# A hybrid decoder on one core: the operands of RWKV's key projection formed in another order, and another order in its recurrence's step

## The chip, the cores and the metric

The kernel runs on one core of a Trainium2 chip. The metric is device time in microseconds (us) of the whole program, median of three runs. The engines are PE (TensorE, matmuls; PEld loads their weights), DVE (VectorE), ACT (ScalarE), POOL (GpSimd) and SP (SyncE, which here only issues DMAs). Each engine takes its instructions in the order of its own queue; a DMA is issued from the queue of SP or ACT and can only be issued when what it waits for has come.

## What is computed

Two decoder layers over x of 1024 tokens by 1024 channels, in float32. The even layer (gMLP and dilated attention) isn't touched. The odd layer is RWKV-7 time mixing:

```python
xx = concat([zeros, h[:, :-1]]) - h
xr, xw, xk, xv, xa, xg = [h + xx * mu[i] for i in range(6)]
r, k, v, g = xr @ w_r, xk @ w_k, xv @ w_v, xg @ w_g
logw = -softplus(-(w0 + tanh(xw @ w1) @ w2)) - 0.5
decay = exp(-exp(logw))
a = sigmoid(a0 + (xa @ a1) @ a2)
kk = hs(k * k_k);  kk = kk * rsqrt(max(sum(kk * kk), 1e-24))     # per head of 64
k = k * (1.0 + (a - 1.0) * k_a)
# per head, over the tokens t:
sa = state @ -kk_t
state = state * w_t + sa (x) (kk_t * a_t) + v_t (x) k_t
y_t = state @ r_t
# then a norm over each head, a bonus sum(r * k * r_k) * v, times silu(g), @ w_o, residual, final norm
```

## The kernel before

Matrices are multiplied in float32 precision by splitting both operands in a high part and a rest (`xh`, `xl`; `wh`, `wl`; the weights' rest is formed by L106, the activations' by L740 on POOL or DVE) and adding three products (`mm3`, L153). The odd layer runs as a plan of twelve chunks `j`: r (j 0 to 3), k (4 to 7), v (8 to 11), each of 256 output columns. r and k are channel-major: a **unit** is one block of 128 channels `p` and one half `f` of 512 tokens, 24 matmuls of 512 columns. v is token-major, 768 matmuls of 256 columns. Before a projection its input is mixed (`mixed`: a scale on ACT L736, one operation on DVE L737, the high part on ACT, the rest L740). `mixed_out` does the same for the second half of the gate's input and stores it in DRAM; it stands at j = 6 (`XD`), in k's projection.

For every unit of k, `Prep` takes the matmuls' result and forms the operands of the recurrence. Matmuls with the small weights `w2`, `a2` (L795, L796) give the decay and a, tanh is on ACT (L797), a running sum over each chunk of 64 tokens is a scan on DVE (L802), its exponentials `E`, `En` are on ACT. From these and k come `AR` (L809, L811, L812) and `BK` (L813, L814, L817), from k and a the product L816 on POOL and the bonus L820. Two matmuls with a selection matrix `sel` sum over the channels of a head (L822, L823); their result is copied to `so` (L825) and stored in two pieces. AR and BK go to DRAM. In this part of the program a scheduler sets the order within each engine.

The recurrence works in chunks of 64 tokens (`c`), two per step (block `b`): 8 blocks, of which a start, six steps and an end are written out by hand as lists of names (`SCAN_START`, `SCAN_STEP`, `SCAN_END`); for all engines and SP the order is then that of the lists. What the names issue: `U` solves for a chunk (PE, copied by ACT to UV, L1250); `st` multiplies into the state (PE L1271) and adds it to S (DVE L1273); `keep` decays S (POOL L1262); `W`, `Y` are the products with the state. Ahead of the step, for later chunks: `ld` loads A and BK; `sc`, `al` form the chunk's score matrices MY, M and AK; `msk` masks MY (L1078) and AK (L1080) on POOL; `dec` decays BK (POOL L1062); `T` transposes it. The triangular inverse of a block is found partly by rows on DVE: `sM` stores M (L1055, issued by ACT), `lM` loads it as Nt in another layout, `ip`, `ia`, `ie` form its diagonal blocks, each count of `ib` issues one piece of its rows (L1153 to L1160), `ic` stores the rows as XT (L1167, SP), `lX` loads them as X (L1175, SP), and `mx`, `ma`, `mb` merge them on PE (L1193, L1206). `uv` loads v into UV, `Yd` stores Y (L1298, issued by ACT). `g` issues a piece of the gate projection (PE L943), stored to `sg_d` (L950).

Of the kernel before, what the change touches and what calls it, by code (L numbers as in the profile page):

```python
# [42 lines left out]
XD = 6  # L43
# [712 lines left out]


class Prep:


    def __init__(self, g, a, pool):
# [3 lines left out]
        self.w2 = {}  # L765

    def second(self, p):

        if p not in self.w2:
            g, nc = self.g, self.g.nc  # L770
            self.w2 = {p: []}
            for n in ("rw_w2", "rw_a2"):
# [8 lines left out]
        return self.w2[p]

    def __call__(self, p, f, pk):
        g, nc, pool = self.g, self.g.nc, self.pool
        sl = slice(f * 512, (f + 1) * 512)
        kk, rk = g.pr[:, 8, p:p + 1], g.pr[:, 10, p:p + 1]
        c3 = lambda t: t.rearrange("p (c t) -> p c t", t=CH)
        ks = pool.tile([P, 512], F32, name="ks", bufs=2)
        nc.scalar.activation(ks, pk, AF.Copy)  # L789
# [4 lines left out]
        for i, ((wh, wl), src, b) in enumerate(zip(self.second(p), (self.TH, self.UA), (g.w0h, g.a0h))):  # L794
            nc.tensor.matmul(pz[:, i], wh, src[:, sl], start=True, stop=False)  # L795
            nc.tensor.matmul(pz[:, i], wl, src[:, sl], start=False, stop=True)  # L796
# [3 lines left out]
        L = pool.tile([P, 512], F32, name="L", bufs=2)  # L800
        E = tw
        nc.vector.tensor_tensor_scan(L, g.smask.rearrange("p c t -> p (c t)"), tw, 0.0, op0=OP.mult, op1=OP.add)  # L802
# [6 lines left out]
        nc.vector.scalar_tensor_tensor(AR[:, :, 0, 1:CH], c3(ks)[:, :, 1:CH], kk, E3[:, :, 0:CH - 1],  # L809
                                       op0=OP.mult, op1=OP.mult)  # L810
        nc.vector.tensor_scalar(AR[:, :, 0, 0:1], c3(ks)[:, :, 0:1], kk, None, op0=OP.mult)  # L811
        (nc.vector if p % 2 else nc.gpsimd).tensor_tensor(AR[:, :, 1, :], c3(rt), E3, OP.mult)  # L812
        nc.vector.scalar_tensor_tensor(BK[:, :, 0, :], c3(ta), 1.0, c3(ks), op0=OP.add, op1=OP.mult)  # L813
        nc.vector.scalar_tensor_tensor(BK[:, :, 0, :], BK[:, :, 0, :], g.kkn[:, p:p + 1], En, op0=OP.mult, op1=OP.mult)  # L814
        nc.vector.tensor_scalar(ta, ta, g.kah[:, p:p + 1], g.kam[:, p:p + 1], op0=OP.mult, op1=OP.add)
        nc.gpsimd.tensor_tensor(ta, ta, ks, OP.mult)  # L816
# [3 lines left out]
        nc.vector.scalar_tensor_tensor(ta, rt, rk, ta, op0=OP.mult, op1=OP.mult)  # L820
        pss = g.bC([64, 512], "pt")
        nc.tensor.matmul(pss[0:32], g.sel, sq, start=True, stop=True)  # L822
        nc.tensor.matmul(pss[32:64], g.sel, ta, start=True, stop=True)  # L823
        so = pool.tile([64, 512], F32, name="so", bufs=1)
        nc.vector.tensor_copy(so, pss)  # L825
        nc.sync.dma_start(g.ss_d[:, p, sl], so[0:2])
        nc.sync.dma_start(g.bo_d[:, p, sl], so[32:34])
# [4 lines left out]


def odd_layer(g, a, hT, wt, out):
# [34 lines left out]
    mixed(g, hT, 0, (1,), xn)  # L869
    for j, (i, W, fn, ld, ev, c) in enumerate(plan):  # L870
        if c == 0:
# [11 lines left out]
        if j == XD:  # L883
            mixed_out(g, hT, 5, 1, g.xg_d)
# [676 lines left out]
```

## Time and profile before

| | us |
|---|---|
| median of three runs | 1486.93 (1485.79 to 1487.78) |
| the profiled execution | 1486.46 |
| its span, from the first to the last recorded instruction | 1484.4 |
| PE busy in the span | 1305.9 |
| DVE, ACT, POOL busy | 913.4, 628.8, 544.7 |

Busy time says how much of the span an engine worked, not what it was waiting for. The odd layer lies after about 640 us: r to 728, k with its operands to about 938, v to 997, the start of the recurrence to 1082, six steps with U at 1082.7, 1121.6, 1158.3, 1192.0, 1228.0 and 1263.9, and the end.

### The profile page before, as it was taken

How to read it: one execution, taken by the hardware profiler on the slowest of the kernel's cores; microseconds unless marked ns; L12 is line 12 of the kernel's file. 1: busy time of each engine (PE TensorE's matmuls, PEld its weight loads, DVE VectorE, ACT ScalarE, POOL GpSimd, SP SyncE). 2: the span in 40 equal slices, each digit the busy share in tenths (PEclk: the TensorE clock that was granted, in tenths of full speed). 3: DMA queues.
4: the chain of work that ended last, by engine and by line, in shares of the span. 5: the costliest groups of instructions: out<-in, count | busy, mean ns of one | idle time of the engine just before them, and what ended most of it. 6: DMA issues, size and time to landing. Idle time of an engine off the chain costs nothing.

```text
span 1484.4 us, 30909 instructions
## 1 busy us (share of the span) xinstructions
PE 1305.9 (88%) x12773; PEld 1110.6 (75%) x12773; DVE 913.4 (62%) x1489; ACT 628.8 (42%) x1188; POOL 544.7 (37%) x353
## 2 busy tenths in 40 slices
PE   5899999799998999999998869998977878687877
PEld 5887788788896799978854537896766667567877
DVE  8741536663556436760698997332676776668884
ACT  4421535543554324652555554232434444354322
POOL 8750102030213512221343353023744444367751
PEclk9999999899999999999999989998988998889999
DMA  6277446240543435133187547427675565675412
GB/s 220 86 265 188 114 128 171 72 128 15 148 108 115 141 106 152 47 110 108 50 243 196 132 118 196 105 74 218 167 234 157 154 156 145 160 220 212 145 34 95
DMA packets 253276, 209.16 MB, mean 141 GB/s; under 512 B 79648, under 2 KB 215424, under 8 KB 253136
## 3 DMA queue, kind: packets, MB, share of 16 engines
q1 hardware_dynamic: 230336, 191.98, 44.4%
q10 hardware_dynamic: 22800, 15.21, 3.7%
q8 instruction: 100, 1.64, 0.5%
q14 instruction: 40, 0.33, 0.1%
HBM read 135.71 MB, written 71.43 MB: 140 GB/s over the span
## 4 chain that ended last, share of the span: by engine, by line
PE 51%; DVE 17%; DMA 12%; ACT 7%; issue 6%; POOL 4%; SPq 2%; ACTq 1%; DVEq 0%; POOLq 0%
PE pj L153 33%; PE pj L943 3%; PE pt L572 2%; PE pj L1473 2%; PE pj L711 2%; DMA X<-XT 1%; DMA XT<-xm 1%; DMA w<-in_rw_a_dram 1%; DMA BK<-BK_d 1%; PE ch L1271 1%; PE op L580 1%; ACT wh L105 1%; PE sp L559 1%; PE sp L562 1%; ACT UV L1250 1%
## 5 line engine op out<-in xcount | busy, mean ns | idle before, releaser
L106 POOL TENSOR_TENSOR wl<-wraw,wh 128x1024 fp32r<-128x1024 f32 x38 | 95.6, 2518 | 174.2 <-ACT wh L105 161.5
L153 PE MATMUL pj<-hh,wh 128*128 128x512 f32 x320 | 127.3, 398 | 0.0
L153 PE MATMUL pj<-hh,wl 128*128 128x512 f32 x320 | 126.7, 396 | 0.0
L153 PE MATMUL pj<-hl,wh 128*128 128x512 f32 x320 | 126.6, 396 | 0.0
L106 DVE TENSOR_TENSOR wl<-wraw,wh 128x1024 fp32r<-128x1024 f32 x46 | 71.7, 1564 | 84.7 <-ACT wh L105 44.0
L105 ACT ACTIVATE wh<-wraw 128x1024 fp32r<-128x1024 f32 x84 | 88.2, 1057 | 66.0 <-DMA wraw<-in_w_in_even_dram 23.3
L153 PE MATMUL pj<-xl,wh 128*128 128x512 f32 x256 | 104.2, 408 | 2.5 <-DVE xl L740 2.5
L153 PE MATMUL pj<-xh,wh 128*128 128x512 f32 x256 | 103.8, 408 | 2.5 <-ACT ks L789 2.5
L153 PE MATMUL pj<-xh,wl 128*128 128x512 f32 x256 | 103.6, 405 | 0.2 <-POOL wl L106 0.2
L566 DVE CUSTOM_DVE_ANT_0 sc<-sp,tb 128x128 f32<-128x128 f32 (+3 forms) x64 | 48.2, 754 | 58.0 <-PE sp L562 49.6
L1473 PE MATMUL pj<-wh,yl 128*128 128x256 f32 x256 | 74.1, 289 | 6.4 <-POOL yl L106 6.4
L1473 PE MATMUL pj<-wh,yh 128*128 128x256 f32 x256 | 74.8, 292 | 5.2 <-DVE x L1477 5.2
L153 PE MATMUL pj<-wh,hh 128*128 128x256 f32 x256 | 74.7, 295 | 2.9 <-ACT hh L265 2.6
L737 DVE SCALAR_TENSOR_TENSOR xm<-hT,pr,xm 128x512 f32<-128x512 f32 x56 | 49.0, 917 | 44.1 <-ACT xm L736 43.7
L153 PE MATMUL pj<-wh,hl 128*128 128x256 f32 x256 | 74.8, 293 | 1.2 <-DVE hl L266 1.2
L153 PE MATMUL pj<-wh,yl 128*128 128x256 f32 x256 | 73.8, 288 | 1.9 <-POOL yl L624 1.9
L153 PE MATMUL pj<-wl,hh 128*128 128x256 f32 x256 | 74.3, 291 | 0.0
L1473 PE MATMUL pj<-wl,yh 128*128 128x256 f32 x256 | 73.8, 288 | 0.0
L153 PE MATMUL pj<-wh,yh 128*128 128x256 f32 x256 | 73.3, 286 | 0.5 <-ACT yh L623 0.5
L153 PE MATMUL pj<-wl,yh 128*128 128x256 f32 x256 | 72.9, 285 | 0.0
L153 PE MATMUL pj<-wh,xh 128*128 128x256 f32 x256 | 72.2, 282 | 0.1
L153 PE MATMUL pj<-wl,xh 128*128 128x256 f32 x256 | 72.2, 282 | 0.0
(320 smaller groups left out, 4063.2 us busy)
## 6 DMA issues: line engine op xcount, KB each, us to landing
wraw<-in_w_in_even_dram SPq DMA_DIRECT2D x28, 512.0 KB
tb<-tb SPq DMA_DIRECT2D x16, 512.0 KB
A_d<-AR SPq DMA_DIRECT2D x16, 512.0 KB
wraw<-in_rw_wg_dram SPq DMA_DIRECT2D x16, 512.0 KB
A<-A_d SPq DMA_DIRECT2D x16, 512.0 KB
BK<-BK_d SPq DMA_DIRECT2D x16, 512.0 KB
xt<-in_x_dram SPq DMA_DIRECT2D x8, 512.0 KB
dv<-vt SPq DMA_DIRECT2D x16, 256.0 KB
```

The source lines that it names most:

```text
L105: nc.scalar.activation(hi, raw, AF.Copy)
L106: sub.tensor_tensor(lo, raw, hi.bitcast(F32), OP.subtract)
L153: nc.tensor.matmul(ps, a(k), b(k), start=(n == 0), stop=(n == 3 * KT - 1))
L559: nc.tensor.matmul(sp[:, c0:c1], qs[:, b * P:(b + 1) * P], kh[:, c0:c1], start=True, stop=False)
L562: nc.tensor.matmul(sp[:, c0:c1], qs[:, b * P:(b + 1) * P], kl[:, c0:c1], start=False, stop=True)
L566: nc.vector.tensor_tensor_reduce(sc[:, :n], sp[:, :n], tb[:, off:off + n], 1.0, BIG, OP.add, OP.min, mn)
L572: nc.tensor.transpose(pt[:, j - j0, :], sc[:, j * P:(j + 1) * P], g.ident)
L580: nc.tensor.matmul(op[:, s0:QW], vt[:, j, :], pth[j // 4][:, j % 4, s0:QW], start=(j == 0), stop=False)
L711: nc.tensor.matmul(ps, x[:, 2 * kk + i, :], y[:, i, o:o + 512], start=(n == 0), stop=(n == 47))
L737: nc.vector.scalar_tensor_tensor(t, hT[kk, f][:, j, 0:512], g.pr[:, i, k:k + 1], t, op0=OP.mult, op1=OP.add)
L943: nc.tensor.matmul(ps, u[:, k], v[:, k % 2], start=(k == 0 and i == 0), stop=(k == KT - 1 and i == 2))
L1473: nc.tensor.matmul(ps[:, i, :], u[:, k], v[:, k % 4], start=(k == 0 and j == 0), stop=(k == KT - 1 and j == 2))
```

## The change

*In k's projection.* The small weights are loaded and split once for a chunk of 256 columns, and each unit's call is divided: `gates` (matmuls, tanh, scan, exponentials, the parts of BK that need no k) is issued ahead of the unit's own matmuls, `operands` after them, and `sum`, the two matmuls with `sel`, after the matmuls of the next unit. `sel` is wider and is shifted by p, so that the sums of all eight p add up in one bank per half and are copied and stored once. E has a leading column of ones, so that AR's first column needs no operation of its own; two operations move to ACT (bias and scale); the product of k with En becomes POOL's. For j = 4 to 7 the order on PE is that of the code. `mixed_out` moves to v's chunks, two of eight parts after each.

*In the recurrence.* `msk` is divided: `mA` (AK, this block's chunks) and `mY` (MY, two chunks later in the program than before). The rows of the inverse stand ahead of the second state update. M's and Y's stores are issued by SP. v is loaded a chunk earlier. The gate's pieces stand at other places.

```diff
-    "U0 al0 ib2 st0 al1 sM0 uv0 Y0 keep1 ib1 W1 sc0 ib1 U1 uv1 ld6 st1 sc1 ib1 ic0 dec0 Y1 lM0 W2 keep2 ip0 lX0 "
-    "gx1 sc2 Yd0 T0 msk0 g2 ia0 sc3 g2 mx0 ma0 ie0 g2 dec1 T1 mb0 msk1 g3 ib3 ld7 gl2")
+    "U0 al0 ib2 st0 al1 Y0 uv1 keep1 mA0 mA1 W1 sM0 sc0 ib3 ld6 U1 sc1 g1 mY0 mY1 ic0 st1 dec0 lM0 Y1 g1 W2 keep2 "
+    "ip0 lX0 gx1 uv2 sc2 Yd0 T0 g1 sc3 ia0 ld7 mx0 ma0 dec1 ie0 g2 mb0 g2 T1 g2 ib3 gl2")
...
+    def project(self, x, w, c, fs=(0, 1)):
...
+                t = self.gates(2 * c + m, f)
+                ps = g.bA([P, 512], "pj")
+                mm3(g.nc, ps, lambda k: wh(k, m), lambda k: wl(k, m),
+                    lambda k: x[0][k // 2, f][:, k % 2, 0:512], lambda k: x[1][k // 2, f][:, k % 2, 0:512])
+                self.sum()
+                self.operands(2 * c + m, f, ps, *t)
...
-        nc.vector.scalar_tensor_tensor(AR[:, :, 0, 1:CH], c3(ks)[:, :, 1:CH], kk, E3[:, :, 0:CH - 1],
-                                       op0=OP.mult, op1=OP.mult)
-        nc.vector.tensor_scalar(AR[:, :, 0, 0:1], c3(ks)[:, :, 0:1], kk, None, op0=OP.mult)
-        (nc.vector if p % 2 else nc.gpsimd).tensor_tensor(AR[:, :, 1, :], c3(rt), E3, OP.mult)
-        nc.vector.scalar_tensor_tensor(BK[:, :, 0, :], c3(ta), 1.0, c3(ks), op0=OP.add, op1=OP.mult)
-        nc.vector.scalar_tensor_tensor(BK[:, :, 0, :], BK[:, :, 0, :], g.kkn[:, p:p + 1], En, op0=OP.mult, op1=OP.mult)
-        nc.vector.tensor_scalar(ta, ta, g.kah[:, p:p + 1], g.kam[:, p:p + 1], op0=OP.mult, op1=OP.add)
-        nc.gpsimd.tensor_tensor(ta, ta, ks, OP.mult)
-        nc.vector.tensor_tensor(BK[:, :, 1, :], c3(ta), En, OP.mult)
...
+        nc.scalar.activation(BK[:, :, 0, :], ta.rearrange("p (c t) -> p c t", t=CH), AF.Identity,
+                             bias=g.kkn[:, p:p + 1], scale=g.kkn[:, p:p + 1])
+        nc.scalar.activation(ta, ta, AF.Identity, bias=g.kam[:, p:p + 1], scale=g.kah[:, p:p + 1])
...
+        kt = pool.tile([P, 512], F32, name="kt", bufs=1)
...
+        nc.gpsimd.tensor_tensor(BK[:, :, 1, :], c3(ks), c3(En), OP.mult)
+        nc.gpsimd.tensor_tensor(kt, ta, ks, OP.mult)
+        nc.vector.scalar_tensor_tensor(AR[:, :, 0, :], c3(ks), kk, E[:, :, 0:CH], op0=OP.mult, op1=OP.mult)
+        nc.vector.scalar_tensor_tensor(kt, rt, rk, kt, op0=OP.mult, op1=OP.mult)
+        (nc.vector if p % 2 else nc.gpsimd).tensor_tensor(AR[:, :, 1, :], c3(rt), E[:, :, 1:CH + 1], OP.mult)
+        nc.vector.tensor_tensor(BK[:, :, 0, :], BK[:, :, 0, :], BK[:, :, 1, :], OP.mult)
+        nc.vector.tensor_tensor(BK[:, :, 1, :], c3(ta), BK[:, :, 1, :], OP.mult)
...
+        nc.tensor.matmul(ps[0:32], g.sel[:, 7 - p:39 - p], sq, start=p == 0, stop=p == KT - 1)
+        nc.tensor.matmul(ps[32:64], g.sel[:, 7 - p:39 - p], ta, start=p == 0, stop=p == KT - 1)
...
+            order.enter_context(tc.manual_schedule(engines={mybir.EngineType.PE}))
...
-        if j == XD:
-            mixed_out(g, hT, 5, 1, g.xg_d)
...
+        if j >= 8:
+            mixed_out(g, hT, 5, 1, g.xg_d, (2 * j - 16, 2 * j - 15))
...
-            self.g.nc.scalar.dma_start(self.g.MA_d[b2][k].rearrange("c q t s -> t (c q) s"),
+            self.g.nc.sync.dma_start(self.g.MA_d[b2][k].rearrange("c q t s -> t (c q) s"),
...
-            self.g.nc.scalar.dma_start(self.g.Y_d[b].rearrange("(c t) h d -> t c h d", c=2)[:, :, 8 * e:8 * e + 8],
+            self.g.nc.sync.dma_start(self.g.Y_d[b].rearrange("(c t) h d -> t c h d", c=2)[:, :, 8 * e:8 * e + 8],
```

DVE's queue in the middle of k's projection, before: the operations of one unit, whose factors are in `tz_7465` and `L_7487`, from the first scaling to the bonus (numbers behind names are buffers).

```order
L799 TENSOR_SCALAR tz_7465<-tz_7465 128x512
L825 COPY so_7427<-pt_7424 64x512
L802 SCALAR_TENSOR_TENSOR L_7487<-smask_4820,tz_7465 128x512
L813 SCALAR_TENSOR_TENSOR BK_7493<-tz_7465,ks_7460 128x8x64
L815 TENSOR_SCALAR tz_7465<-tz_7465,kah_4810,kam_4812 128x512
L809 SCALAR_TENSOR_TENSOR AR_7492<-ks_7460,pr_4802,tz_7465 128x8x63
L812 TENSOR_TENSOR AR_7492<-rl_7462,tz_7465 128x8x64
L811 TENSOR_SCALAR AR_7656<-ks_7624,pr_4802 128x8
L779 TENSOR_TENSOR rw_w2l_7714<-w2_7710,rw_w2h_7713 128x128
L814 SCALAR_TENSOR_TENSOR BK_7493<-BK_7493,kkn_4808,L_7487 128x8x64
L817 TENSOR_TENSOR BK_7493<-tz_7465,L_7487 128x8x64
L820 SCALAR_TENSOR_TENSOR tz_7465<-rl_7462,pr_4802,tz_7465 128x512
```

The same engine and stretch, after: the unit whose factors are in `tz_7212`, with its AR in `AR_7259`, its BK in `BK_7224` and its bonus in `kt_7258`.

```order
L814 TENSOR_SCALAR tz_7212<-tz_7212 128x512
L842 TENSOR_TENSOR BK_7162<-tz_7150,BK_7162 128x8x64
L815 SCALAR_TENSOR_TENSOR tz_7212<-smask_4820,tz_7212 128x512
L839 SCALAR_TENSOR_TENSOR kt_7196<-rl_7147,pr_4802,kt_7196 128x512
L840 TENSOR_TENSOR AR_7259<-rl_7209,E1_6010 128x8x64
L838 SCALAR_TENSOR_TENSOR AR_7259<-ks_7254,pr_4802,E1_6010 128x8x64
L841 TENSOR_TENSOR BK_7224<-BK_7224 128x8x64
L814 TENSOR_SCALAR tz_7283<-tz_7283 128x512
L842 TENSOR_TENSOR BK_7224<-tz_7212,BK_7224 128x8x64
L815 SCALAR_TENSOR_TENSOR tz_7283<-smask_4820,tz_7283 128x512
L839 SCALAR_TENSOR_TENSOR kt_7258<-rl_7209,pr_4802,kt_7258 128x512
```

The unit's bonus product now stands behind the scaling and the scan of the next unit (`tz_7283`), and its AR and BK take four operations where they took seven.

DVE's queue in the recurrence's step, before, from the step's first row pieces (products of Nt and the rows found so far, and their sums) to the last, around the two state updates S:

```order
L1153 TENSOR_TENSOR tm<-Nt,xm 128x864
L1155 TENSOR_REDUCE R<-tm 128x3x12
L1273 TENSOR_TENSOR S<-ch,S 128x512
L1153 TENSOR_TENSOR tm<-Nt,xm 128x864
L1155 TENSOR_REDUCE R<-tm 128x3x12
L1153 TENSOR_TENSOR tm<-Nt,xm 128x576
L1155 TENSOR_REDUCE R<-tm 128x2x12
L1273 TENSOR_TENSOR S<-ch,S 128x512
L1158 TENSOR_TENSOR tm<-DN,R 128x768
L1160 TENSOR_REDUCE xm<-tm 128x12x8
```

And after:

```order
L1199 TENSOR_TENSOR tm<-Nt,xm 128x864
L1201 TENSOR_REDUCE R<-tm 128x3x12
L1319 TENSOR_TENSOR S<-ch,S 128x512
L1199 TENSOR_TENSOR tm<-Nt,xm 128x864
L1201 TENSOR_REDUCE R<-tm 128x3x12
L1199 TENSOR_TENSOR tm<-Nt,xm 128x576
L1201 TENSOR_REDUCE R<-tm 128x2x12
L1204 TENSOR_TENSOR tm<-DN,R 128x768
L1206 TENSOR_REDUCE xm<-tm 128x12x8
L1319 TENSOR_TENSOR S<-ch,S 128x512
```

The second update of S has moved from ahead of the last row piece to behind it.

SP's queue in one step, before: the loads of v, then A and BK, the rows' store and the loads of the inverse.

```order
L1013 DMA UV<-v_d 64x512 x4
L1001 DMA A<-A_d 128x1024
L1003 DMA BK<-BK_d 128x1024
L1167 DMA XT_139<-xm 1024x1x32 x2
L1095 DMA Nt<-MA_132 64x1024 x2
L1175 DMA X<-XT_139 32x16x32 x4
L1001 DMA A<-A_d 128x1024
L1003 DMA BK<-BK_d 128x1024
```

And after:

```order
L1055 DMA UV<-v_d 64x512 x2
L1097 DMA MA_132<-M 32x16x32 x4
L1043 DMA A<-A_d 128x1024
L1045 DMA BK<-BK_d 128x1024
L1213 DMA XT_139<-xm 1024x1x32 x2
L1141 DMA Nt<-MA_132 64x1024 x2
L1221 DMA X<-XT_139 32x16x32 x4
L1055 DMA UV<-v_d 64x512 x2
L1344 DMA Y_146<-Y 64x2x512 x2
L1043 DMA A<-A_d 128x1024
L1045 DMA BK<-BK_d 128x1024
```

M's and Y's stores now stand in this queue; v's loads are parted, and the second of them and Y's store stand behind X.

More of the change, by code (lines that the diff above doesn't have):

```diff
@@ L41 @@
 NT = 4
-XD = 6
 GR = 9
@@ L741, in mixed, with mixed_out @@
             xh[kk, f], xl[kk, f] = h, l
-def mixed_out(g, hT, i, f, dst):
+def mixed_out(g, hT, i, f, dst, ks):
     nc = g.nc
-    for k in range(KT):
+    for k in ks:
         src = hT[k // 2, f][:, k % 2]
@@ L783, in __call__ @@
-    def __call__(self, p, f, pk):
-        g, nc, pool = self.g, self.g.nc, self.pool
[L785 to L789, printed above, removed]
+        self.E = [pool.tile([P, 8, CH + 1], F32, name=f"E{i}") for i in range(2)]
+        for E in self.E:
+            g.nc.vector.memset(E[:, :, 0:1], 1.0)
@@ new lines, in __init__, with second @@
+        self.w2, self.sums, self.n = {}, {}, 0
+        self.due = None
+    def second(self, c):
+        if c not in self.w2 and c < D // CB:
+            g, nc = self.g, self.g.nc
+            raw = g.s2([P, 2, CB], F32, "w2")
+            for i in range(2):
+                for j, n in enumerate(("rw_w2", "rw_a2")):
+                    nc.sync.dma_start(raw[64 * i:64 * i + 64, j], self.a[n][0][:, c * CB:(c + 1) * CB])
+            hi = self.pool.tile([P, 2, CB], F32R, name="w2h", bufs=2)
+            lo = self.pool.tile([P, 2, CB], F32R, name="w2l", bufs=2)
+            nc.scalar.activation(hi, raw, AF.Copy)
+            nc.vector.tensor_tensor(lo, raw, hi.bitcast(F32), OP.subtract)
+            self.w2[c] = hi, lo
@@ new lines, in project @@
+    def project(self, x, w, c, fs=(0, 1)):
+        g = self.g
+        wh, wl = w
+        self.second(c)
+        for f in fs:
+            for m in range(2):
+                t = self.gates(2 * c + m, f)
[4 more added lines that the diff above has]
+                self.operands(2 * c + m, f, ps, *t)
+            if f == 0:
+                self.second(c + 1)
@@ L790, in __call__, with gates @@
+    def gates(self, p, f):
+        g, nc, pool = self.g, self.g.nc, self.pool
+        sl, o = slice(f * 512, (f + 1) * 512), slice((p % 2) * P, (p % 2 + 1) * P)
+        wh, wl = self.w2[p // 2]
         rt = pool.tile([P, 512], F32, name="rl", bufs=2)
@@ L793, in __call__ @@
         tz = pool.tile([P, 2, 512], F32, name="tz", bufs=2)
[L794 to L796 removed]
+        for i, (src, b) in enumerate(((self.TH, g.w0h), (self.UA, g.a0h))):
+            nc.tensor.matmul(pz[:, i], wh[:, i, o], src[:, sl], start=True, stop=False)
+            nc.tensor.matmul(pz[:, i], wl[:, i, o], src[:, sl], start=False, stop=True)
             nc.scalar.activation(tz[:, i], pz[:, i], AF.Tanh, bias=b[:, p:p + 1], scale=0.5)
@@ L821, in __call__ @@
[L821 to L827, printed above, removed]
+        nc.vector.tensor_tensor_scan(tw, g.smask.rearrange("p c t -> p (c t)"), tw, 0.0, op0=OP.mult, op1=OP.add)
@@ L831, in __call__, with sum @@
             nc.sync.dma_start(g.BK_d[64:128, f * 8:(f + 1) * 8, p, 1 - j], BK[64:128, :, j])
+    def sum(self):
+        if self.due is None:
+            return
+        g, nc = self.g, self.g.nc
+        (p, f, sq, ta), self.due = self.due, None
+        if p == 0:
+            self.sums[f] = g.bC([64, 512], "pt")
+        ps = self.sums[f]
+        nc.tensor.matmul(ps[0:32], g.sel[:, 7 - p:39 - p], sq, start=p == 0, stop=p == KT - 1)
+        nc.tensor.matmul(ps[32:64], g.sel[:, 7 - p:39 - p], ta, start=p == 0, stop=p == KT - 1)
+        if p == KT - 1:
+            sl = slice(f * 512, (f + 1) * 512)
+            so = g.s2([64, 512], F32, "xm")
+            nc.vector.tensor_copy(so, ps)
+            nc.sync.dma_start(g.ss_d.rearrange("e q s -> (e q) s")[:, sl], so[0:16])
+            nc.sync.dma_start(g.bo_d.rearrange("e q s -> (e q) s")[:, sl], so[32:48])
 def odd_layer(g, a, hT, wt, out):
@@ L869, in odd_layer @@
     mixed(g, hT, 0, (1,), xn)
+    order = ExitStack()
     for j, (i, W, fn, ld, ev, c) in enumerate(plan):
+        if j == 3:
+            prep.second(0)
+        if j == 4:
+            order.enter_context(tc.manual_schedule(engines={mybir.EngineType.PE}))
+        if j == 8:
+            prep.sum()
+            order.close()
         if c == 0:
@@ L1073, in transposed, with mask_AK, mask_MY @@
                 nc.scalar.activation(BKT[:, 4 * q:4 * q + 4], pt, AF.Copy)
-    def masks(self, c):
+    def mask_AK(self, c):
+        nc, t = self.g.nc, self.T[c]
+        for r in (slice(0, 64), slice(64, 128)):
+            nc.gpsimd.affine_select(t["AK"][r], t["AK"][r], pattern=[[0, KT], [1, CH]], compare_op=OP.is_ge, fill=0.0,
+                                    base=-1, channel_multiplier=-1)
+    def mask_MY(self, c):
         nc, t = self.g.nc, self.T[c]
```

58 lines of the change are left out of this document (23 added, 35 removed), and 18 rows, old and new, of tables (SCAN_END, SCAN_START).

## The prediction

> **What bounds the kernel now.** I read the page first, then the odd layer stretch by stretch, then what PE waits for in k's projection, then one recurrence step as a chain in order of time.
>
> ```profile
> PE 1305.9 (88%) x12773; PEld 1110.6 (75%) x12773; DVE 913.4 (62%) x1489; ACT 628.8 (42%) x1188; POOL 544.7 (37%) x353
> 732.00:940.00 208.00, 179.20 (x773) 121.82 (x772) 184.04 (x238) 111.96 (x197) 87.80 (x60) 0.93 0.65 173
> 940.00:997.30 57.30, 57.30 (x480) 56.34 (x479) 15.21 (x16) 16.49 (x35) 6.09 (x4) 1.00 0.18 49
> 1082.00:1285.00 203.00, 159.38 (x4663) 135.70 (x4663) 140.91 (x215) 83.59 (x146) 85.35 (x84) 0.91 0.59 154
> 941.37 55.91 PE pj L153 x473
> ```
>
> PE is busy 88% of the span, but the average hides two stretches where others set the pace. The second to fourth rows give, after the length, the busy time of PE, weight loads, DVE, ACT and POOL. In k's projection (732 to 940) PE is busy 179 of 208 us and DVE 184, DVE and POOL together 272. From 941.37, the chain says, 473 matmuls of v run without a pause, 0.118 us each. In the recurrence (1082 to 1285) PE is busy 159 of 203, so nothing is full and a chain of waits sets the period.
>
> In k's stretch DVE and POOL block each other. Start, duration, engine, line:
>
> ```profile
> 801.44 1.28 DVE L811 TENSOR_SCALAR AR<-ks,pr 128x8 f32<-128x8 f32 x1
> 802.63 1.83 DVE L814 SCALAR_TENSOR_TENSOR BK<-BK,kkn,L 128x512 f32<-128x512 f32 x1
> 804.38 0.73 DVE L809 SCALAR_TENSOR_TENSOR AR<-ks,pr,tz 128x504 f32<-128x504 f32 x1
> 802.65 1.26 POOL L816 TENSOR_TENSOR tz<-tz,ks 128x512 f32<-128x512 f32 x1
> ```
>
> The DVE operation at 802.63 takes 1.83 us, where its fellow at 804.38 takes 0.73; the difference is what POOL's product, started 0.02 us later, holds. So I count what each operation takes undisturbed, the first of three durations (min/median/max, ns):
>
> ```profile
> L737 DVE SCALAR_TENSOR_TENSOR xm<-hT,pr,xm x20: 737/741/1794, 731.9 to 873.8; 128x512 f32<-128x512 f32 x20
> L799 DVE TENSOR_SCALAR tz<-tz x14: 393/414/1634, 761.1 to 928.5; 128x512 f32<-128x512 f32 x14
> L802 DVE TENSOR_TENSOR_SCAN L<-smask,tz x14: 1204/1222/2314, 762.8 to 928.9; 128x512 f32<-128x512 f32 x14
> L812 DVE TENSOR_TENSOR AR<-rl,tz x8: 676/683/1785, 739.6 to 932.1; 128x512 f32<-128x512 f32 x8
> L816 POOL TENSOR_TENSOR tz<-tz,ks x16: 1262/1672/2478, 743.9 to 934.8; 128x512 f32<-128x512 f32 x16
> L740 POOL TENSOR_TENSOR xl<-xm,xh x12: 1287/1660/2187, 732.2 to 876.3; 128x512 fp32r<-128x512 f32 x12
> L106 POOL TENSOR_TENSOR wl<-wraw,wh x7: 2366/2475/2924, 746.3 to 923.4; 128x1024 fp32r<-128x1024 f32 x7
> L106 DVE TENSOR_TENSOR wl<-wraw,wh x7: 1194/1212/2018, 754.3 to 926.1; 128x1024 fp32r<-128x1024 f32 x7
> ```
>
> Counted so, DVE's 238 less 15 copies out of PSUM come to 142 us; neighbours overlap by 0.07 us (801.44 + 1.28 ends after 802.63), which leaves 127. POOL's come to 67. That is 194 of 208, 93%: the two together bound this stretch.
>
> One step, from the chain in order of time:
>
> ```profile
> 1122.18 0.60 ACT UV L1250
> 1127.17 0.53 ACTq L1055
> 1131.77 0.59 ACT UV L1250
> 1133.01 2.00 PE ch L1271 x32
> 1135.11 0.69 DVE S L1273
> 1136.70 0.96 DVE xm L1160
> 1137.68 0.55 SPq L1167
> 1138.28 2.91 DMA XT<-xm
> 1142.77 4.60 DMA X<-XT
> 1147.41 1.91 PE pt L1193 x62
> 1153.75 1.17 PE pt L1206 x64
> 1154.91 2.28 PE pj L943 x9
> 1158.32 0.59 ACT UV L1250
>   PE ch L1271: 26.2, 7
> L1250 ACT ACTIVATE UV<-ch x28: 581/592/593, 1082.7 to 1312.6; 64x512 f32<-64x512 f32 x28
> ```
>
> The last inverse row (L1160) stands in DVE's queue behind the state update S (L1273) of the second chunk, which waits for PE; only then are the rows stored (XT), loaded in another layout (X) and merged (L1193, L1206), after which the next step's U can come. The row "PE ch L1271" sums DVE's idle time in front of S: 26.2 us in seven waits, 3.7 each. This loop, from 1121.57 to 1158.32 here, is what sets the step.
>
> **The change, part by part.** *k's projection.* After it, from the first mixing of the stretch to the last operand of v's second half, DVE has 56 operations of the 0.74 kind (24 mixings, 16 AR, 16 bonus), 52 of 0.68 (12 residuals, 40 products), 3 weight splits of that size, 16 scans of 1.20, 16 of 0.39, 4 weight residuals of 1.19: 41.4 + 35.4 + 2.0 + 19.2 + 6.2 + 4.8 = 109 us, less 139 × 0.07 = 99. POOL has 40 products of 1.26, 12 residuals of 1.29 and 4 of 2.37: 75. Sum 174 against 194. (POOL's 16 copies of eight elements are left out in both sums.) Gone are 16 eight-element operations, 32 of the operand operations (ACT forms them with a bias and a scale), 14 of 16 copies of sums, 28 of 32 small weight splits. ACT gains two operations per unit, 32 at the 0.6 of the UV rows above, 19 us on 112 of 208: hidden. Eight mixings for the gate go to v's stretch, where DVE works 15 and POOL 6 of 57 us: hidden; their stores are counted at the recurrence's start. The row of matmuls and sums on PE is the same in number, so PE's 179 + 57 us stay.
>
> The Trainium skill's page "SBUF — State Buffer", section "Who interferes with whom", states that a DVE instruction with two SBUF inputs and a GpSimd instruction that reads SBUF exclude each other for the whole instruction, whoever starts first. The rows at 802 agree. By that rule the product that goes from DVE to POOL is a loss of 16 × (1.26 − 0.68) = 9 us, an estimate already inside the sum above; if the engines did not share, it would be a gain.
>
> The group begins where this one does now:
>
> ```profile
> 729.20 3.40 DVE L737 SCALAR_TENSOR_TENSOR xm<-hT,pr,xm 128x512 f32<-128x512 f32 x5
> ```
>
> With the pair filled as before, 93%, v's second half has its operands at 729 + 174/0.93 = 916; filled wholly, at 903. I take the middle, 910. Of v's 768 matmuls 96 are done before that; 672 × 0.118 = 79 us follow without a pause, as in the quoted row. v ends at 989 where it now ends at 997.3: **−8** (bounds −15 and −2). In the old order v's matmuls fill PE's gaps in k; the new fixed order lets none in, so every gap left in k is paid in full, which is why 20 us less work brings only 8.
>
> *Recurrence, start.* SP now stores the last operands of the gate ahead of the first BK loads; Nt's load no longer stands after a gate store.
>
> ```profile
> 1003.63 6.78 DMA BK<-BK_d
> 1019.69 6.42 DMA sg_d<-XT
> ACT rt L1196 <- DMA BK<-Y: 8.0, 1, 8.0
> ```
>
> The second piece is 6.4 us on the chain, and may go whole. The first is a load on the chain too: four stores of half its size ahead of it can cost up to half of 6.8, about 3. I take **−2** (−6 to +3).
>
> *Step.* All remaining inverse rows now precede the second S, so DVE's 26.2 us leave the XT path: −26.2. What comes instead: the AK masks move beside these rows, and POOL and DVE block each other there too.
>
> ```profile
> 1145.52 0.66 POOL L1080 TENSOR_SCALAR_AFFINE_SELECT AK<-AK 64x512 f32<-64x512 f32 x1
> 1146.44 1.79 DVE L1127 TENSOR_TENSOR tm<-DN 128x36 f32<-128x36 f32 x1
> 1286.99 0.20 DVE L1127 TENSOR_TENSOR tm<-DN 128x36 f32<-128x36 f32 x1
> ```
>
> The same operation takes DVE 1.79 us at 1146, beside POOL, and 0.20 at 1287, where POOL has no masks. I take one mask of 0.66 per step, in the seven steps of the waits: +4.6 (bounds 0, and three masks, +14, one for each product of the rows). The MY masks in turn leave the diagonal operations; that I set at nothing, since the loop above doesn't pass through them (its bound is one such delay, 1.6 per step). Between the merge and U one gate piece more runs on PE, three of the nine matmuls of the 2.28 row: 6 × 0.8 = +4.8. M's and Y's stores go from ACT to SP: ACT's issue (the 0.53 row, one of four) delayed W there and now leaves; on SP they stand with the A and BK loads ahead of XT, 512 KB each. XT's store would be issued 3.0 us sooner (3.7 less 0.7), and the two issues of M's stores on SP lie in front of it in time; that its transfer queues there is rival B. The loads of v for U come a chunk earlier, which costs nothing as long as their three buffers come free. Sum: −26.2 + 4.6 + 4.8 = **−17** (bounds −26, with the rows undisturbed and the gate piece hidden, and −7, with three masks), 2.8 per step.
>
> *End.* ACT's wait of 8.0 us on an unrelated transfer lies beside the same merge; it may go or come back as another. Nothing, bounds −8 and +2.
>
> Total −8 − 2 − 17 = −27 on the profiled execution's 1486.46 (span 1484.4 + 2.06), which is 0.5 below the median 1486.93; on the median, 1460.
>
> **Rivals.** *A, the pair doesn't bind k.* If DVE and POOL only slow each other, the new order runs k at PE's rate and PE's idle time there, 208 − 179.2 = 28.8, goes whole: 1487 − 29 − 2 − 17 = 1439. For it: 20 us less work. Against it: the 802 rows.
>
> *B, X stays where it is.* The XT store is earlier but waits on SP's queue behind A and BK, or X's load meets the same transfers. Each us costs six steps; at 2.4 us later than I assume the step keeps only 0.4 us, and the time is 1487 − 8 − 2 − 2 = 1475. For it: DMA takes 2.91 + 4.60 us of the chain in the quoted step. Against: the same A and BK loads stand ahead of XT on SP today.
>
> *C, slower: k's fixed order.* On PE the two sums of a unit now stand between its successor's matmuls and the next gates, and nothing passes them. The bonus product kt reaches them through a POOL product (one kt buffer) and a DVE operation queued behind the next unit's scan.
>
> ```profile
> PE pt L823 <- DVE tz L820: 7.3, 3, 3.6
> ```
>
> Today three such waits cost PE 7.3 us, 2.4 each. Were all 15 paid with DVE and POOL idle too, 36 us come on top of 903: v ends at 903 + 36 + 79 = 1018, +21, and the total is 1487 + 21 − 2 − 17 = 1489. It decides from 2.3 us per unit. For it: the strict order. Against: 24 matmuls, 5.7 us by the 0.118 row (half as wide), lie between.
>
> **How the numbers follow.** My sum 0.53 (own range 1446 to 1473), A 0.12, B 0.20, C 0.10, gains and losses that cancel 0.05. The range 1435 to 1482 takes in A, B and the sum, and leaves out C and the ends of the bounds. A change under 0.2%, 3 us, can't be told from none here. Faster 0.84, same 0.06, slower 0.10.
>
> **What would show it.** Right: v's unbroken run begins near 910 and ends near 989; PE's waits in k are for kt; in the steps no DVE wait for PE stands ahead of the XT store, and U follows U after about 33 us. Wrong: k's units near 8.3 us with PE full (A); XT's landing unchanged after the U (B); PE waits of over 2 us at every pair of sums (C). A new wait on SP ahead of XT, or one for Nt ahead of the diagonal operations, would break the step's term.

## The result, and the profile after

The changed kernel's median is 1480.89 us (nine runs, 1476.05 to 1484.90) against 1487.78 for the kernel before, run beside it; the ratio is 0.9945 with an interval of 0.9927 to 0.9964. It is faster by 0.55%, under a third of what was forecast (1460). The profiled execution took 1478.45, its span 1476.4, which is 8.0 less than before.

Where the 8.0 come from is told by four points in the two traces: the first matmul of the gate's projection (v's end), the first U of the steps, the U after the sixth step, and the end. The three rows are of the kernel after (its line numbers are new: the gate is L985, UV is L1296). The first is a group of matmuls: their count, their shortest, median and longest duration in ns, then the first and the last start, so v ends at 994.1. The other two are the first and the seventh U.

```profile
L985 PE MATMUL pj<-xh,wh x15: 388/393/398, 994.1 to 1003.8; 128*128 128x512 f32 x15
1084.03 1.21 ACT L1296 ACTIVATE UV<-ch 64x512 f32<-64x512 f32 x2 [0.49 <-PE ch L1292]
1292.91 1.20 ACT L1296 ACTIVATE UV<-ch 64x512 f32<-64x512 f32 x2 [4.40 <-PE ch L1267]
```

The same of the kernel before:

```profile
L943 PE MATMUL pj<-xh,wh x15: 388/394/400, 997.1 to 1006.9; 128*128 128x512 f32 x15
1082.71 1.21 ACT L1250 ACTIVATE UV<-ch 64x512 f32<-64x512 f32 x2 [2.07 <-PE ch L1246]
1304.68 1.20 ACT L1250 ACTIVATE UV<-ch 64x512 f32<-64x512 f32 x2 [4.16 <-PE ch L1221]
```

| stretch, us | before | after | difference | forecast |
|---|---|---|---|---|
| up to v's end | 997.1 | 994.1 | −3.0 | −8 |
| recurrence's start, to the first U | 85.6 | 89.9 | +4.3 | −2 |
| six steps | 222.0 | 208.9 | −13.1 | −17 |
| from there to the end | 179.7 | 183.5 | +3.8 | 0 |
| sum | 1484.4 | 1476.4 | −8.0 | −27 |

No single term accounts for the miss: each came out 4 to 6 us worse than forecast. The page's first row and a window of k's projection (length, then busy PE, weight loads, DVE, ACT, POOL) show the work that went:

```profile
PE 1283.8 (87%) x12773; PEld 1097.6 (74%) x12773; DVE 869.3 (59%) x1401; ACT 647.3 (44%) x1192; POOL 566.1 (38%) x369
741.00:902.00 161.00, 125.24 (x465) 81.67 (x465) 124.88 (x121) 97.90 (x148) 77.73 (x61) 0.92 0.57 153
```

The same window before:

```profile
741.00:902.00 161.00, 132.89 (x488) 84.93 (x486) 147.89 (x191) 87.62 (x149) 70.71 (x48) 0.90 0.65 174
```

DVE works 23 us less in these 161, as the change meant, and PE works 7.7 us **less** too: it is idle for 36 us where it was idle for 28. What it waits for from 736 to 902 (us in total, times, longest):

```profile
PE pz L810 <- ACT tz L812: 34.4, 15, 7.3
PE pt L859 <- DVE kt L839: 2.7, 1, 2.7
```

All but 2.7 us is one wait, and not the one that the third rival named (kt). In the same stretch of the kernel before, where the scheduler put v's matmuls and others in between, this wait was:

```profile
PE pz L795 <- ACT tz L797: 4.7, 3, 2.8
```

One instance of it in the kernel after, PE's row and the rows of ACT ahead of it:

```profile
753.27 0.79 PE L810 MATMUL pz<-UA,w2h 128*128 128x512 f32 x1 [5.70 <-ACT tz L812]
750.29 1.06 ACT L104 ACTIVATE wh<-wraw 128x1024 fp32r<-128x1024 f32 x1 [0.69 <-DMA wraw<-in_rw_wk_dram]
751.25 0.58 ACT L831 ACTIVATE ks<-pj 128x512 f32<-128x512 f32 x1
751.92 0.72 ACT L833 ACTIVATE sq<-ks,pr 128x512 f32<-128x512 f32 x1
752.55 0.67 ACT L812 ACTIVATE tz<-pz,w0h 128x512 f32<-128x512 f32 x1
754.53 0.69 ACT L812 ACTIVATE tz<-pz,a0h 128x512 f32<-128x512 f32 x1 [1.31 <-PE pz L811]
```

In `gates` the loop issues two matmuls and then their tanh, twice. Both pairs write one tile `pz`, so the second pair waits until ACT has read the first half, though it writes the other half. ACT comes to this tanh only behind the weights' high part (L104), k's copy and its square. The 24 matmuls of the unit stand behind the second pair.

### The profile page after: what moved, and what is told of

It is laid out like the page before. It is cut to its first block, busy times and chain, and to the rows that moved or that the text cites. A ratio compares the mean times of both kernels' runs of the same rounds, so it can differ in the third digit from the quotient of the medians.

```text
span 1476.4 us, 30738 instructions
## 1 busy us (share of the span) xinstructions
PE 1283.8 (87%) x12773; PEld 1097.6 (74%) x12773; DVE 869.3 (59%) x1401; ACT 647.3 (44%) x1192; POOL 566.1 (38%) x369
## 4 chain that ended last, share of the span: by engine, by line
PE 55%; DVE 16%; DMA 10%; ACT 7%; issue 6%; POOL 3%; SPq 2%; ACTq 0%; DVEq 0%; POOLq 0%
PE pj L152 35%; PE pj L985 3%; PE pj L1519 2%; PE pt L571 2%; PE pj L710 2%; DMA kl<-dk 1%; ACT wh L104 1%; PE sp L558 1%; PE sp L561 1%; DMA BK<-BK_d 1%; DVE rt L197 1%; PE py L1327 1%; DMA w<-in_rw_a_dram 1%; DVE wl L105 1%; PE op L579 1%
## 5 line engine op out<-in xcount | busy, mean ns | idle before, releaser
L105 POOL TENSOR_TENSOR wl<-wraw,wh 128x1024 fp32r<-128x1024 f32 x38 | 92.4, 2438 | 215.1 <-ACT wh L104 191.8
L104 ACT ACTIVATE wh<-wraw 128x1024 fp32r<-128x1024 f32 x84 | 88.2, 1057 | 76.4 <-DMA wraw<-in_w_in_even_dram 25.3
L152 PE MATMUL pj<-wh,xl 128*128 128x256 f32 x256 | 71.8, 280 | 0.0
```

What stands on the lines that cost most here:

```text
L105: sub.tensor_tensor(lo, raw, hi.bitcast(F32), OP.subtract)
L152: nc.tensor.matmul(ps, a(k), b(k), start=(n == 0), stop=(n == 3 * KT - 1))
```

## The experiments

Ratios are to the kernel before, run beside each group; they are compared rather than medians, since the groups ran on different chips.

### The two parts apart

`k_only` has the change in k's projection (and the gate's mixing in v), `scan_only` that in the recurrence, each with the other part as before.

> Only the change in k's projection (with the gate's mixing moved to v), the recurrence's lists, masks and stores as before. Theory 1, from the two traces: k and v end 3 us earlier (994 against 997), and the start of the recurrence gives this back, because BK's first loads stand behind the gate's stores on SP and come at the same 1004: no change, 1487 within 2 us. Theory 2, the forecast's term: v ends 8 us earlier and this arrives: about 1479.

Measured: 1490.24 against 1489.45, ratio 1.0012 (0.9994 to 1.0031). Alone, the projection's part brings nothing that can be seen. In its trace v ends at 995.2 and the first U comes at 1081.1, each under 2 us earlier than before.

> Only the change in the recurrence, k's projection as before. Theory 1, from the two traces: six steps 13 us shorter, the end 4 us longer, Nt's load at the start up to 4 us later, so 5 to 9 us less: 1478 to 1482. Theory 2, the forecast's terms: 17 to 19 us less, 1469.

Measured: 1476.82, ratio 0.9923 (0.9897 to 0.9949). Its six steps take 204.0 us (from the first and seventh U, 1086.7 and 1290.7), 18 less than before, the size of the forecast's step term. Its start takes 88.3 us from v's end (998.4) against 85.6, and from the seventh U to the end 183.6 against 179.7. The recurrence's part carries the whole gain, and its start and end give a third of it back.

### k's projection: the wait for the tanh

`pz_first` takes the wait away by issuing both pairs of matmuls first:

```diff
             nc.tensor.matmul(pz[:, i], wl[:, i, o], src[:, sl], start=False, stop=True)
+        for i, b in enumerate((g.w0h, g.a0h)):
             nc.scalar.activation(tz[:, i], pz[:, i], AF.Tanh, bias=b[:, p:p + 1], scale=0.5)
```

> The changed kernel, but both pairs of gate matmuls are issued ahead of both tanh, so that the second pair doesn't wait for ACT's tanh of the first. Theory 1: this wait, 34 us of PE in 15 units of k, is what sets k's pace; PE's units go from about 9.9 to 8.5 us, v ends at 975 to 980 instead of 994, and the whole is 10 to 15 us under the changed kernel. Theory 2: DVE and POOL's shared time sets the pace; the wait only changes its name (to the bonus kt, or to k's copy), v ends no earlier than 990, and the whole gains under 4 us.

Measured: 1459.49, ratio 0.9805 (0.9779 to 0.9830), some 21 us under the changed kernel. The waits of PE in k, the gate's first matmul, and the last residuals of v's input, on POOL and DVE, in its trace:

```profile
PE pt L860 <- DVE kt L840: 10.9, 4, 4.4
PE pj L152 <- DVE xl L739: 5.1, 1, 5.1
PE pt L859 <- ACT sq L834: 5.0, 1, 5.0
L986 PE MATMUL pj<-xh,wh x18: 391/396/795, 971.5 to 999.2; 128*128 128x512 f32 x18
L739 POOL TENSOR_TENSOR xl<-xm,xh x8: 1382/1666/1781, 859.5 to 893.6; 128x512 fp32r<-128x512 f32 x8
L739 DVE TENSOR_TENSOR xl<-xm,xh x8: 678/680/1719, 864.5 to 895.8; 128x512 fp32r<-128x512 f32 x8
```

v ends at 971.5 instead of 994.1, 22.6 earlier, and the whole gain of 20.6 in the profiled spans (1476.4 to 1455.8) follows from it. Theory 1 named the place and was too small on the size. The waits for kt and sq are now 16 us: the third rival's mechanism exists, at less than half of its price. With the tanh's wait gone, the forecast's way to v's end holds: PE's last pause in k, for v's residuals, ends at 894.2; 118 of v's matmuls are done by then, and the other 650 at 0.118 us would end at 970.9.

`pe_free` instead leaves PE's order in k to the scheduler:

```diff
-            order.enter_context(tc.manual_schedule(engines={mybir.EngineType.PE}))
+            pass
```

> The changed kernel without the fixed order on PE in k's projection. Theory 1: the fixed order lets the wait for the first tanh stand as idle PE time; with a free order other matmuls go between and v ends 8 to 20 us earlier: 1460 to 1472. Theory 2: the dependence of the second gate pair on the tanh is what costs, and a free order has nothing ready to put there until v's inputs are mixed: within 4 us of the changed kernel.

Measured: 1481.03, ratio 0.9945 (0.9927 to 0.9962), the changed kernel's. Its PE waits in k are other ones, and v ends 3.5 us later, at 997.6:

```profile
PE pt L859 <- DVE kt L839: 10.8, 5, 3.8
PE pz L810 <- ACT tz L812: 7.1, 4, 3.5
L985 PE MATMUL pj<-xh,wh x16: 387/392/793, 997.6 to 1019.2; 128*128 128x512 f32 x16
```

The wait for the tanh is down from 34.4 to 7.1 us and nothing is gained. From 729 to v's end PE still idles 33 us, where it idles 37 in the changed kernel, and it is busy 236 us instead of 228; the granted clock up to 902 is 0.90 there and 0.92 in the changed kernel, behind it 0.95 and 1.00. So freeing the order doesn't bring the time back; `pz_first`, which keeps the order and takes away the dependence, does.

`dve_prod` tests the shared time of DVE and POOL on top of `pz_first`:

```diff
-        nc.gpsimd.tensor_tensor(BK[:, :, 1, :], c3(ks), c3(En), OP.mult)
+        nc.vector.tensor_tensor(BK[:, :, 1, :], c3(ks), c3(En), OP.mult)
```

> The kernel with both gate pairs first, and in addition the product of k with En on DVE instead of POOL. Theory 1, DVE and POOL exclude each other and their shared time now sets k's pace: 16 x (1.26 - 0.68) = 9 us less of it, so k and v end 3 to 8 us earlier than with the gate pairs alone. Theory 2, DVE's own queue sets it (AR, both BK products and the bonus in a row behind the scan): 16 x 0.6 = 10 us more of DVE, k and v end 3 to 8 us later.

Measured: 1464.77, ratio 0.9820 (0.9796 to 0.9845) against 0.9805: no faster; its first U comes at 1065.1 against 1063.2. Neither theory's size is there. Counted from the starts and ends of the rows, DVE or POOL is at work in 166 of the 171 us from the group's first mixing to v's last residual in `pz_first` (725.8 to 896.5), and in 157 of 170 in `dve_prod` (728.2 to 897.8). So 9 us less of shared time shortened the stretch by only 1: in `pz_first` the pair was all but full, and something else set the pace when it had less to do. The longer queue of DVE, theory 2, may be that; no run parts the two.

### The start: the gate's stores, and M's store on SP

`mix_early`:

```diff
-        if j >= 8:
-            mixed_out(g, hT, 5, 1, g.xg_d, (2 * j - 16, 2 * j - 15))
+        if j in (8, 9):
+            mixed_out(g, hT, 5, 1, g.xg_d, range(4 * j - 32, 4 * j - 28))
```

> The changed kernel, but the gate's mixing stands in v's first two chunks (four parts after each) instead of all four. Theory 1: the start of the recurrence waits for these stores on SP; BK's first loads come 3 to 4 us earlier (1000 to 1001) and the whole is 3 to 4 us shorter. Theory 2: the start is bound by Nt's load behind the transfers on SP, and nothing moves by more than 1 us.

Measured: 1471.80, ratio 0.9890 (0.9863 to 0.9918), 8 us under the changed kernel, more than either theory. v ends 2.6 us later than there (996.7), yet BK's load is issued 1.0 earlier (1003.1 against 1004.1), Nt is there 2.2 earlier (1030.9 against 1033.1) and the first U 3.8 earlier (1080.2); the six steps take 203.1 against 208.9. Only the 2.2 at Nt can be traced to the edit. Behind Nt even equal lists scatter: from Nt to the first U it is 53.3 us in the kernel before and 48.7 in `rows_only` (below), whose start is the same. In the six profiles with the same steps and end (the changed kernel, `pz_first`, `mix_early`, `sm_start`, `dve_prod`, `pe_free`) the steps range from 203.1 to 214.9. The granted clock in them is highest, 0.90, in the shortest and lowest, 0.86, in the longest; but 0.87 goes with 209.1 and 0.89 with 211.2, so this is part of the reason at most, and the rest isn't shown.

`sm_start` lets ACT issue M's first store, as before, and only that:

```diff
-            self.g.nc.sync.dma_start(self.g.MA_d[b2][k]
+            (self.g.nc.sync if b2 else self.g.nc.scalar).dma_start(self.g.MA_d[b2][k]
```

> The changed kernel, with M's first store issued by ACT again, all others by SP. Theory 1: in the start SP stands in front of M's store until M is there, so the gate weights and A and BK behind it are issued 6 to 8 us later and lie in front of Nt's load; with ACT issuing, Nt lands at 1029 to 1030 instead of 1033 and the first U comes about 4 us earlier. Theory 2: Nt waits for M's own transfer; nothing moves by more than 1 us.

Measured: 1477.84, ratio 0.9921 (0.9898 to 0.9944); the first U comes at 1080.9, 3.1 earlier. SP's queue and DVE's wait in the changed kernel:

```profile
1016.15 1.96 SPq L1097 DMA_DIRECT2D MA<-M  x4
1018.21 1.13 SPq L970 DMA_DIRECT2D wraw<-in_rw_wg_dram  x2
1022.94 1.09 SPq L1141 DMA_DIRECT2D Nt<-MA  x2
1033.12 1.16 DVE L1163 TENSOR_TENSOR DN<-Nt,rn 128x256 f32<-128x256 f32 x1 [31.14 <-DMA Nt<-MA]
```

and in `sm_start`:

```profile
1010.83 1.58 SPq L970 DMA_DIRECT2D wraw<-in_rw_wg_dram  x2
1020.21 6.64 SPq L1141 DMA_DIRECT2D Nt<-MA  x2
1029.99 2.54 DVE L1163 TENSOR_TENSOR DN<-Nt,rn 128x256 f32<-128x256 f32 x1 [27.80 <-DMA Nt<-MA]
```

SP stood in front of M's store until M was there; two gate weights of 512 KB behind it were issued at 1018 instead of 1011 and lay ahead of Nt. With the store on ACT, Nt is there 3.1 us earlier, at 1030.0 against 1033.1. The median's gain, 3 us, is within what the runs of the changed kernel spread.

Counted from v's end, Nt's data are there after 32.3 us in the kernel before, whose row is this,

```profile
1029.44 2.61 DVE L1117 TENSOR_TENSOR DN<-Nt,rn 128x256 f32<-128x256 f32 x1 [29.82 <-DMA Nt<-MA]
```

and after 39.0 in the changed kernel, 35.7 in `sm_start`, 34.2 in `mix_early` and 36.2 in `k_only`. So the gate's stores in v and M's store on SP each make it 3 to 5 us later.

### The end: a store behind an unrelated transfer

In both kernels ACT stops ahead of X's last merge. After:

```profile
1274.33 0.63 ACT L991 ACTIVATE XT<-pj 128x512 f32<-128x512 f32 x1
1283.26 0.33 ACTq L992 DMA_DIRECT2D sg_d<-XT  x1
1283.64 0.60 ACT L1073 ACTIVATE MY<-pm 128x512 f32<-128x512 f32 x1 [8.67 <-DMA lnw<-in_rw_lnw_dram]
```

The gate's store waits until the load of `lnw` is through (issued at 1276.45, landed 6.74 later, at 1283.19); before, it was the load BK<-Y (8.0 us, the row in the prediction). They share no data. What they share is the semaphore that tells of their landing: each DMA here has one of eight, used in turn, and by the semaphore events of the traces the store has that of `lnw` in the changed kernel and that of BK<-Y in the kernel before. `sg_sp` has SP issue this one store:

```diff
-        g.nc.scalar.dma_start(g.sg_d[n % KT, :, f * 512:(f + 1) * 512], t)
+        (g.nc.sync if n == 13 else g.nc.scalar).dma_start(g.sg_d[n % KT, :, f * 512:(f + 1) * 512], t)
```

> The changed kernel, with one of the gate's stores (the one that ACT issues ahead of the last merge) issued by SP. In both kernels ACT stands 8 us in front of this store, behind a transfer that has nothing to do with it, and X's merge stands behind the store. Theory 1: the merge was ready, so U of the last part comes about 8 us earlier (1284 to 1286 instead of 1293) and the whole is 5 to 8 us shorter than the changed kernel. Theory 2: the merge would wait for X's load at that time anyway, or the end waits for its other loads: under 2 us.

```profile
1280.68 0.63 ACT L991 ACTIVATE XT<-pj 128x512 f32<-128x512 f32 x1
1281.15 0.65 ACT L1073 ACTIVATE MY<-pm 128x512 f32<-128x512 f32 x1
1291.69 1.20 ACT L1296 ACTIVATE UV<-ch 64x512 f32<-64x512 f32 x2 [5.67 <-PE ch L1292]
```

Measured: 1477.18, ratio 0.9906 (0.9882 to 0.9931). ACT's stop is gone, and the sixth step takes 30.2 us instead of 37.3; but SP issues the store only at 1293.20, behind loads of `w_o`, and from the seventh U to the end it is 186.6 instead of 183.5. Of the 7 us some 4 remain in these two stretches, between the two theories. For the whole no gain is shown: the interval overlaps that of the changed kernel, and the profiled execution, 1480.37, is no shorter than the changed kernel's 1478.45.

### The step: the rows alone, XT's place, the stores

`rows_only` is the kernel before with nothing but the order of the rows:

```diff
-    "U0 al0 ib2 st0 al1 sM0 uv0 Y0 keep1 ib1 W1 sc0 ib1 U1 uv1 ld6 st1 sc1 ib1 ic0 dec0
+    "U0 al0 ib2 st0 al1 sM0 uv0 Y0 keep1 W1 sc0 ib3 U1 uv1 ld6 sc1 ic0 st1 dec0
```

> The kernel before, with one edit: in the recurrence's step the last inverse row pieces and XT's store are issued ahead of the second state update (its masks, stores and loads stay as they were). Theory 1, the forecast's step term: DVE's wait for PE leaves XT's path; six steps take 12 to 20 us less than their 222, total about 1472. Theory 2: the rows alone don't help, as M's stores on ACT and the masks on POOL stay in the way; the steps gain under 6 us.

Measured: 1472.59 (1464.97 to 1478.44), ratio 0.9889 (0.9863 to 0.9915): 17 us, as much as the step's term of the forecast, and over twice what the whole change brought. Its six steps take 204.8, by the first and the seventh U:

```profile
1077.65 1.21 ACT L1250 ACTIVATE UV<-ch 64x512 f32<-64x512 f32 x2 [0.87 <-PE ch L1246]
1282.44 1.20 ACT L1250 ACTIVATE UV<-ch 64x512 f32<-64x512 f32 x2 [3.88 <-PE ch L1221]
```

The profiled execution is the fastest of the six, 1464.97, and the granted clock in its steps is 0.93 against 0.88 in the kernel before. How much of the steps' 17 us goes with the clock isn't shown; in the changed kernel the rows' move comes with 13 us less at 0.89. DVE's idle time in front of S is still there in the changed kernel (first row) and in this one (second), but XT no longer stands behind it:

```profile
  PE ch L1317: 32.0, 9
```

```profile
  PE ch L1271: 13.7, 7
```

`scan_act` is `scan_only` with M's and Y's stores issued by ACT again (`nc.scalar` in `store_M` and `store_Y`).

> The recurrence's change alone, with M's and Y's stores issued by ACT as before. The rows' order alone gained 17 us, the whole of the recurrence's change 11 to 13. Theory 1: the stores on SP give the rest back (the first U 4 us later in the start, where SP stands in front of M): about 1472, the first U at 1082 instead of 1087. Theory 2: the divided masks beside the rows and the other places of the gate's pieces give it back: 1476 to 1479, with the steps no shorter than the 204 us of the recurrence's change alone.

Measured: 1474.33, ratio 0.9899 (0.9877 to 0.9922). The first U comes at 1081.5 instead of 1086.7, as theory 1 said; Nt is there 32.8 us after v's end instead of 36.4. The steps take 207.5 instead of 204.0. The intervals of this ratio, of `scan_only`'s and of `rows_only`'s overlap: that M's store on SP makes Nt later at the start is shown, that the rest of the lists costs or gains anything isn't.

`combo_xt` and `combo_free` start from the four edits together (below). The first puts XT's store ahead of the loads of A and BK (`ib3 ic0 ld6 U1` for `ib3 ld6 U1`, and `ic0` gone from its old place); the second frees PE's order as in `pe_free`.

> The four edits at once, and in the step XT's store ahead of the loads of A and BK on SP. Theory 1 (rival B of the forecast): in the long steps XT's transfer queues behind A and BK (6.5 us instead of 3); with XT ahead each step is 1 to 3 us shorter, 1430 to 1439. Theory 2: A and BK then come later and the next scores wait; no change or up to 6 us more.

> The four edits at once, without the fixed order on PE in k. Theory 1: PE is still idle some 20 us in k (waits for the bonus and the residuals), which v's first matmuls can fill: 5 to 10 us shorter, 1435 to 1440. Theory 2: v's inputs come too late in k to fill anything, and the free order delays k's own matmuls: the same or up to 10 us longer.

Measured: 1448.60, ratio 0.9720 (0.9700 to 0.9740), and 1454.69, ratio 0.9772 (0.9747 to 0.9797), against 0.9701 for the four edits. Neither helps; the free order costs some 10 us. In a long step of the changed kernel XT's transfer is issued right behind A and BK and takes 6.51 us on the chain (first row), where it took 2.9 to 4.3 before; in the four edits together the chain has 5.5 to 6.9. With XT ahead, in `combo_xt`, it has 4.21 (second row) and 3.55:

```profile
1166.82 6.51 DMA XT<-xm
```

```profile
1172.67 4.21 DMA XT<-xm
```

So A and BK ahead of it do make it longer. But putting XT ahead didn't shorten the whole, nor the six steps (202.4 us against 200.0).

### The edits together

> The changed kernel with four edits at once: both gate pairs first, the gate's mixing in v's first two chunks, M's first store and one gate store moved as in the runs beside it. If their gains add (21 and 9 us as measured, 4 and 7 as expected of the two others), 1440. If the start is bound by the same load in several of them, the second and third give 5 together: 1446 to 1450.

Measured: 1444.73, ratio 0.9701 (0.9679 to 0.9722). By the ratios, the gains against the changed kernel, 21, 8, 6 and 4 us, would add to 39; together they are 36.

> The kernel before with the projection's change, both gate pairs first, the gate's mixing early, the one gate store on SP, and in the recurrence the rows' order alone (stores on ACT, masks and lists else as before). Theory 1: the rows' order alone is worth 4 to 6 us more than the whole recurrence's change, and this adds to the other edits: 1438 to 1442. Theory 2: the first store on ACT and the end's stall are already mended in the four edits (1444.7), so nothing is left: 1444 to 1449.

Measured: 1443.07 (1440.95 to 1443.49), ratio 0.9683 (0.9660 to 0.9706). It is the fastest here, 3.2% under the kernel before, with the row order alone in the recurrence. Its interval overlaps that of `combo`: the difference between the two lists isn't shown.

## Why the prediction was right or wrong

The direction was right and the sum was wrong: −27 forecast, −8 in the profile.

- **k's projection, −8, measured −3.** The failed step is "the row of matmuls and sums on PE is the same in number, so PE's 179 + 57 us stay", and with it v's end as the time of the pair and 672 matmuls behind it. The number did stay, but the list of what PE waits for was taken from the old order. There the row for this very wait was small (the tanh ahead of the second gate pair, 4.7 us in three waits), because other matmuls stood between; in the new order it came 15 times, 34.4 us. The text did say that every gap left in k is paid in full, and put none in. Taking the wait away moved v's end by 22.6 us. With it there, PE and not the pair sets k's pace: DVE or POOL is at work in 197 of the 209 us up to k's last operand in the kernel before (729.2 to 937.9), 94%, as the sum said, but in 167 of 191 up to v's last residual in the changed kernel (725.0 to 916.4), 87%. DVE waits 19.2 us there, in ten waits, for ACT's copy of k, which comes behind PE's matmuls.
- **v's matmuls.** The sum has 96 of them done by 910; 56 were, and 40 × 0.118 = 5 us is the term's miss. It is the same miss: v's residuals came at 916.4, at the late end of the sum's bounds, but PE has no pause from 891.0 to v's end. They held nothing up, and what PE lost earlier in k was all that counted.
- **The shared time of DVE and POOL** as a bound is borne out where the wait is gone: in `pz_first` the pair is at work 97% of its stretch. The floor of 903 was 6.5 us too late: the group begins at 725.8 there instead of 729, and takes 171 us where the sum has 174. (That sum lists 147 operations of DVE and takes off the overlap of 139; this is 0.6 us.) The Trainium skill's page "SBUF — State Buffer" ("Who interferes with whom") states the exclusion for a DVE instruction with two SBUF inputs and a GpSimd instruction that reads SBUF; the rows at 802 agree with it. The forecast's 9 us of loss by the moved product aren't borne out: with the product back on DVE the ratio is 0.9820 against 0.9805.
- **Rival A** comes near in its number and not in its way. In `pz_first` v ends 25.6 us earlier than before, where A said 28.8. But PE's idle time didn't go whole: it is 22 us from 724.5 to v's end, after 29 in the kernel before. The rest is that the stretch begins 3 us earlier and that as many matmuls are busy 225 us instead of 240, at a granted clock of 0.97 against 0.94.
- **Rival C** named the fixed order on PE, and PE did stand idle in it. It was wrong in the wait (kt: 2.7 us in one wait), and freeing the order changed nothing (`pe_free`).
- **The start, −2, measured +4.3.** The failed step is "the second piece is 6.4 us on the chain, and may go whole". Nt's load had waited for the gate's store, but other transfers were in the queue during that wait, and it waits for these now: issued at 1022.9, it is there at 1033.1, 6.7 us later after v's end than before (39.0 against 32.3). The first piece, "about 3", was right: BK's load is issued 10.0 us after v's end instead of 6.5. That M's store on SP holds up what is queued behind it was asked only of the step, not of the start; it is the other 3 us. The bound of +3 was too near.
- **The steps, −17, measured −13.1.** The mechanism held: the rows behind S were on the path, and `rows_only` gains with them alone. The size was off in the first term: the row of 26.2 us has seven waits, and the seventh, 3.5 us at 1307.1, lies behind the seventh U, in the end. Six steps have 22.6 of it, and six masks 4.0 instead of 4.6: −22.6 + 4.0 + 4.8 = −13.8. That this meets the measured −13.1 is in part luck, since the nine profiles with the rows ahead of S and the gate's store as before give 203.1 to 214.9, on average 208.3, against 222.0 in the kernel before and 225.4 in `k_only`. Rival B's transfer exists and isn't the price.
- **The end, 0, measured +3.8.** ACT's 8 us stop came back as another (8.67), as the text allowed. The 3.8 go with the end's list, which the sum left out: the three profiles with the old list and the gate's store as before (the kernel before, `k_only`, `rows_only`) take 179.7, 179.7 and 180.5 from the seventh U, the eight with the new list 183.2 to 184.2. It isn't that U comes earlier: it does so by 22 us in `rows_only`. Nor is it the stores on SP, which `scan_act` doesn't have (183.3). Which move in the list it is stays open.

## What to carry to other kernels

When an order is fixed by hand, list again for each engine what it waits for in the new order: a small wait may have been small only because a scheduler had put other work in front of it. In this kernel two halves of one tile were one thing to the waits (34.4 us in 15), so issue both writers before the first reader. Take a sum of waits from the same stretch as the time that it is to shorten. And when a store moves to another queue, ask what stands behind it there at its first use, where its data comes late, not only in the steady loop.

## What the runs showed of the hardware that was not expected

A store issued by ACT stood 8.0 us (before) and 8.67 us (after) behind a load that shares no data with it, each time another load, and each time the one whose landing is told by the store's own semaphore; with the store on SP the stop was gone from ACT. And the same lists don't fix the steps' time: six profiles of them gave 203.1 to 214.9 us for six steps, at granted clocks of 0.86 to 0.90 that only roughly follow. The cause isn't shown.
